# Twelve gate tiles of an encoder layer as six seven-product pairs around a state scan

## The chip, the cores and the metric

The kernel runs on one core of a Trainium2 chip. Its time is the device time of one execution in microseconds; the profile's span, from the first to the last instruction, lies about one microsecond below it. In the profile PE is TensorE's matmuls, PEld its weight loads, DVE is VectorE, ACT ScalarE, POOL GpSimd and SP SyncE, which issues the DMAs here.

## The reference

One encoder layer works on two sequences (prompt and sample) of 512 tokens and width 1024, each with 256 memory tokens, in fp32. Of the layer, this is what matters here:

```python
xn = _rmsnorm(x, p['norm_mix'][l])
h = xn @ p['w_in'][l]
u, q, k, v, xq, g = jnp.split(h, IN_SPLITS, axis=-1)
y_s5 = _s5_branch(u, ...)                      # a scan over time, forward and backward, then a GLU
y_diff = _diff_attention(q, k, v, ...)
y_x = _cross_attention(xq, mk, mv)
for n in range(N_BRANCH):
    term = jax.nn.sigmoid(g[..., n * D_MODEL:(n + 1) * D_MODEL]) * (branches[n] @ p['w_up'][l, n])
    merged = term if merged is None else merged + term
x = x + merged @ p['w_out'][l]
gate, up = jnp.split(_rmsnorm(x, p['norm_ffn'][l]) @ p['w_ffn_in'][l], 2, axis=-1)
return x + (jax.nn.silu(gate) * up) @ p['w_ffn_out'][l]
```

The three gates are 3 x 1024 columns of `h`: 24 tiles of 128 columns, each for 1024 tokens (both sequences) and a contraction over 1024.

## The kernel before

Activations lie with features on the partitions and the 1024 tokens along the free axis. Every fp32 operand is split in a high part that TensorE takes as fp32r and a low part that is the rest (`split`: a copy on ScalarE, line 134, and a subtraction on VectorE, line 135, or 138 with a scale). A product is three matmuls: high by high, high by low, low by high. A tile of 128 output columns for both sequences thus takes 8 (contraction) x 2 (sequences) x 3 = 48 matmuls of 128x512.

The core is one program for a scheduler that orders each engine's instructions at build time: of what is ready, what stands earlier in the program goes first. `issue_after` puts instructions of an engine behind a given one; `PE.on` keeps TensorE in program order (in both attention stages). Before the attention TensorE is free in order, so work that stands later fills waits.

The stages are: memory keys and values; the norm of x, whose split parts `xh[k]`, `xl[k]` (eight each, 1024 tokens) stay until the end of the attention; the projection `u`; the state-space branch (`s5_gen`), the gates around it; the GLU; cross attention; differential attention with its projections; merges; output projection; feed-forward.

Gates: `gates(n)` takes the next n of 24 tiles (`todo`), computes each with `proj`, applies tanh (line 410) and stores it in `gD` (line 411). In the attention stages `gate_units` does the same in pieces of 6 matmuls, from a queue (`queue`, `fill`) that fills the waits for the softmax: `fill(n)` asks for n such matmuls. `NG` and the calls between say how many tiles stand where: 7 ahead of the scan, 3 more, 3 between parts of the scan, 2 between its outputs, 3 behind the GELU (`gates(NG[2])`), 2 in the cross attention, 4 in the differential attention.

The state-space branch is a generator that the main program advances with `next(s5)`. It computes parameters (VectorE), input weights (`input_weights`: products at lines 1551 to 1553, transposes), output weights (`output_weights`: the same products, then matmuls at line 1597 and small stores at 1603 to 1605), the scan's inputs (line 1626), then the scan: 62 steps of four VectorE operations of 128x128 (lines 1641 to 1644), each step on the result of the one before. In the kernel before it yields at the steps in `SCAN`, with a gate's split put between. Behind the scan come four outputs (`x2` copied at 1677 and 1678, matmuls at 1685 to 1687, copies at 1688, eight stores each at 1692), which need the kernels and c from DRAM (`kernels_in`, `c_in`) and the tile `u_`. Then the GELU of the four z tiles (lines 502 to 514), whose tiles lie over those of the branch, and the GLU (lines 525 to 533).

The scheme with seven products in place of eight is in the kernel already, for the feed-forward: `quad_sums` forms four sums of quadrants of the activations (three on VectorE, one on GpSimd), `weights4` four sums of quadrants of two weight tiles on GpSimd (lines 1022 to 1025), and `products` and `quadrants` compute two tiles (gate and up) with seven products of 4 x 3 matmuls and add the results on VectorE out of PSUM (line 1101).

Of the kernel before, what the change touches and what calls it, by code (L numbers as in the profile page):

```python
# [10 lines left out]
F32 = mybir.dt.float32  # L11
# [27 lines left out]

NPREP = (16, 28)  # L40

NG = (7, 6, 3)

NWARM = 13

SCAN = (40, 47, 53, 60)
ROUND = 12582912.0


# [23 lines left out]
def encoder(ctx: ExitStack, tc: tile.TileContext, a, out):  # L73
# [134 lines left out]
    bD = drp.tile([3, 4, P, NT], F32, name="bD")  # L208
    gD = drp.tile([24, P, NT], F32, name="gD")
    mD = drp.tile([4, P, 2, L], F32, name="mD")  # L210
    yD = drp.tile([512, T, NS, NC], F32, name="yD")
    uD = drp.tile([512, T, NS, NC], F32, name="uD")
    kx = Ctx()
# [169 lines left out]
    for t2 in range(2):  # L383
# [9 lines left out]
        for t in range(2):  # L393
            nc.sync.dma_start(uD[(2 * t2 + t) * P : (2 * t2 + t + 1) * P], us[t])

    todo = iter(range(24))

    def behind():
# [3 lines left out]
    def gates(n):  # L402

        for _ in range(n):
            t = next(todo)
            o = proj(a["w_in"][20 + t], xh, xl)
            gt = slot("ld", name="gt")
            for s in range(NS):
                cs = slice(s * L, (s + 1) * L)
                S.activation(out=gt[:, cs], in_=o[s], func=AF.Tanh, scale=0.5)  # L410
            nc.sync.dma_start(gD[t], gt)

    next(s5)
    gates(NG[0])
    next(s5)
    gates(NG[1] + 1 - len(SCAN))
    for i in range(len(SCAN)):
        if i:
            gates(1)
        with tc.issue_after(last_s[1].ins):  # L420
            next(s5)
    for n in (0, 1, 1):
        gates(n)
        with behind():
            next(s5)
    next(s5, None)

    res_ = ExitStack()
# [73 lines left out]
    for t in range(4):  # L502
# [401 lines left out]
    for i in range(-1, n + 3):  # L904
        if i + 1 < n:
            score(i + 1)
        if i == 22:
            queue.insert(1, first_in())
        fill(10 if i < n - 1 else 16)
        if 0 <= i < n:  # L910
            turn(i)
        if 0 < i <= n and steps[i - 1][2] % 2:
            outputs(i - 1)
        fill(10)
        if 1 < i <= n + 1 and steps[i - 2][2] == 3:
            squares(i - 2)
        if i > 2 and steps[i - 3][2] == 3:
            normed(i - 3)
# [42 lines left out]
        nc.sync.dma_start(x1D[m, :, cs], x1[m][:, cs])  # L961
        sum_sq(accs[s], x1[m][:, cs], m == 0)

    last_p = None

    def quad_sums(xa_, xb_, tag="ts", third=PO):

        nonlocal last_p
        b11, b12, b21, b22 = xa_[:, 0:L], xa_[:, L:NT], xb_[:, 0:L], xb_[:, L:NT]
        t_ = slot(tag, [P, 4, L], name="ts")  # L970
        V.tensor_tensor(out=t_[:, 0], in0=b12, in1=b11, op=ALU.subtract)
        last_p = third.tensor_tensor(out=t_[:, 2], in0=b22, in1=b12, op=ALU.subtract)
        V.tensor_tensor(out=t_[:, 1], in0=b22, in1=t_[:, 0], op=ALU.subtract)
        V.tensor_tensor(out=t_[:, 3], in0=b21, in1=t_[:, 1], op=ALU.subtract)
        return t_
# [17 lines left out]
    def operands(i):  # L993
# [6 lines left out]
    H = 4 * P  # L1000

    def weights4(i):

# [406 lines left out]
def s5_gen(k):  # L1410
# [221 lines left out]
            wbs.append(input_weights(3))  # L1632
    for o in range(2, 4):
        output_weights(o)
    yield
    sv = st_t.rearrange("p r g s c -> p r (g s) c")
    l8rv, l8iv = l8r.rearrange("p r g s -> p r (g s)"), l8i.rearrange("p r g s -> p r (g s)")
    for i in range(2, NC):
        p_ = sp.tile([P, 2, G * NS], F32, tag="p_", name="p_")
        q_ = sp.tile([P, 2, G * NS], F32, tag="q_", name="q_")  # L1640
        V.tensor_tensor(out=p_, in0=sv[:, :, :, i - 1], in1=l8rv, op=ALU.mult)
        V.tensor_tensor(out=q_, in0=sv[:, ::-1, :, i - 1], in1=l8iv, op=ALU.mult)
        V.tensor_tensor(out=p_, in0=p_, in1=sv[:, :, :, i], op=ALU.add)
        V.tensor_tensor(out=sv[:, :, :, i], in0=p_, in1=q_, op=ALU.add)
# [147 lines left out]
```

## Time and profile before

| what | value |
|---|---|
| median of three runs | 1603.96 us (1602.52 to 1604.57) |
| profiled execution, span | 1603.0 us, its own time not listed apart |
| TensorE busy | 1587.1 us (99%), 7838 matmuls |
| VectorE busy | 1162.9 us (73%) |
| ScalarE busy | 640.0 us (40%) |
| GpSimd busy | 541.6 us (34%) |
| mean granted clock of TensorE | 0.997 |

A busy TensorE is not one at its peak: matmuls are pipelined, and one that lasts 0.39 us in the profile starts about 0.23 us after the one before it. Idle time of another engine costs nothing unless TensorE waits for it.

### The profile page before, as it was taken

The page shows a single profiled execution, that of the slowest core. Times are in us where ns is not written, and L with a number is a line of the kernel's source. Part 1 is how long each engine was busy: PE and PEld are TensorE (multiplying, and loading weights), DVE is VectorE, ACT ScalarE, POOL GpSimd, SP SyncE. Part 2 cuts the span into 40 slices and gives each one's busy share as a digit, 9 for nine tenths or more (in the row PEclk, how much of TensorE's full clock was granted, in tenths as well). Part 3 has the DMA queues.
Part 4 walks back from the last instruction along what each step waited for, and adds up shares of the span by engine and source line. Part 5 has one row for each costly group of instructions (what it writes and reads, how often), then busy time and mean ns, then how long its engine had stood idle before and what let it go on. Part 6 is the DMA issues. An engine that isn't in the chain of part 4 may idle for free.

```text
span 1603.0 us, 21625 instructions
## 1 busy us (share of the span) xinstructions
PE 1587.1 (99%) x7838; PEld 1314.8 (82%) x7838; DVE 1162.9 (73%) x1856; ACT 640.0 (40%) x1142; POOL 541.6 (34%) x449
## 2 busy tenths in 40 slices
PE   9999999999999999999999999999999999999997
PEld 7888788888898778778878878888888888788877
DVE  7976996076773766776465678888898778988654
ACT  6544323274652455574133443332333323233323
POOL 0010100001333220300343367676665553444653
PEclk9999999999999999999999999999999999999998
DMA  9554523576762111244454432333323223986222
GB/s 366 173 160 150 179 95 125 180 273 201 252 224 102 54 47 40 73 156 140 145 190 132 144 118 80 131 119 129 121 106 118 79 88 119 344 332 198 80 66 106
DMA packets 104891, 237.86 MB, mean 148 GB/s; under 512 B 13520, under 2 KB 45008, under 8 KB 104784
## 3 DMA queue, kind: packets, MB, share of 16 engines
q1 hardware_dynamic: 104784, 236.47, 43.1%
q8 instruction: 62, 1.02, 0.3%
q14 instruction: 45, 0.37, 0.1%
HBM read 165.16 MB, written 71.27 MB: 147 GB/s over the span
## 4 chain that ended last, share of the span: by engine, by line
PE 87%; issue 4%; DVE 3%; DMA 3%; POOL 2%; ACT 0%; SPq 0%; POOLq 0%; DVEq 0%; ACTq 0%
PE bkmm L66 75%; PE bksc L66 3%; PE bktr L66 2%; PE bkoo L66 2%; PE bktr L69 2%; DVE tl L135 1%; PE bktr L1626 1%; POOL mg L793 1%; PE bktr L1597 1%; DMA yt<-bD 1%; PE bktr L1686 0%; PE bktr L1687 0%; PE bktr L1685 0%; PE bktr L1565 0%; DMA acc<-in_w_fo 0%
## 5 line engine op out<-in xcount | busy, mean ns | idle before, releaser
L66 PE MATMUL bkmm<-xh,wh 128*128 128x512 f32 x640 | 255.4, 399 | 0.0
L66 PE MATMUL bkmm<-xh,wl 128*128 128x512 f32 x640 | 250.9, 392 | 0.0
L66 PE MATMUL bkmm<-xl,wh 128*128 128x512 f32 x640 | 250.5, 391 | 0.0
L66 PE MATMUL bkmm<-tl,wh 128*128 128x512 f32 (+1 forms) x621 | 241.2, 388 | 1.4 <-DVE tl L135 1.4
L66 PE MATMUL bkmm<-th,wl 128*128 128x512 f32 (+1 forms) x621 | 241.0, 389 | 0.9 <-DVE wl L135 0.9
L66 PE MATMUL bkmm<-th,wh 128*128 128x512 f32 (+1 forms) x621 | 241.1, 389 | 0.0
L134 ACT CAST wh<-wf 128x1024 fp32r<-128x1024 f32 (+1 forms) x134 | 117.9, 880 | 224.1 <-PE bkmm L66 179.8
L135 DVE TENSOR_TENSOR wl<-wf,wh 128x1024 fp32r<-128x1024 f32 (+1 forms) x134 | 145.1, 1083 | 50.2 <-ACT wh L134 45.7
L66 PEld LDWEIGHTS bkmm<-xh,wh 128*128 128x128 f32 x640 | 120.3, 188 | 30.3 <-issue 7.9
L66 PE MATMUL bkmm<-th,w 128*128 128x512 f32 x432 | 141.5, 392 | 2.7 <-DVE up L1101 1.0
L66 PEld LDWEIGHTS bkmm<-xh,wl 128*128 128x128 f32 x640 | 120.2, 188 | 26.7 <-issue 1.3
L66 PEld LDWEIGHTS bkmm<-xl,wh 128*128 128x128 f32 x640 | 120.4, 188 | 22.4 <-issue 0.4
L66 PEld LDWEIGHTS bkmm<-tl,wh 128*128 128x128 f32 x621 | 116.6, 188 | 25.9 <-DVE tl L135 2.1
L66 PEld LDWEIGHTS bkmm<-th,wl 128*128 128x128 f32 x621 | 116.5, 188 | 25.7 <-DVE wl L135 1.7
L66 PEld LDWEIGHTS bkmm<-th,wh 128*128 128x128 f32 x621 | 116.6, 188 | 23.9
L1165 POOL TENSOR_TENSOR up<-up,acc 128x512 f32<-128x512 f32 x44 | 83.6, 1920 | 87.8 <-DVE up L1101 87.8
L454 POOL TENSOR_TENSOR raw<-raw 128x128 f32<-128x128 f32 x28 | 15.2, 545 | 284.4 <-DVE nb L545 206.5
L66 PEld LDWEIGHTS bkmm<-th,w 128*128 128x128 f32 x432 | 80.9, 188 | 23.8 <-DVE up L1101 3.4
L793 POOL TENSOR_TENSOR mg<-mg,gl 128x1024 f32<-128x1024 f32 x16 | 43.5, 2720 | 139.0 <-DVE gl L789 139.0
L548 ACT ACTIVATE e<-bksc,nb 128x512 f32<-128x512 f32 (+1 forms) x96 | 58.8, 615 | 73.5 <-DVE nb L543 51.9
L66 PE MATMUL bkmm<-tl,w 128*128 128x512 f32 x216 | 84.2, 390 | 0.0
L66 PE MATMUL bkmm<-yh,wh 128*128 128x512 f32 x192 | 75.9, 397 | 0.8 <-ACT wh L134 0.4
(641 smaller groups left out, 3527.8 us busy)
## 6 DMA issues: line engine op xcount, KB each, us to landing
wf<-in_w_in SPq DMA_DIRECT2D x40, 512.0 KB, 3.9
wD<-hl SPq DMA_DIRECT2D x28, 512.0 KB, 2.9
w<-wD SPq DMA_DIRECT2D x28, 512.0 KB, 5.0
gD<-gt SPq DMA_DIRECT2D x24, 512.0 KB, 2.8
gl<-gD SPq DMA_DIRECT2D x24, 512.0 KB, 3.4
wf<-in_w_fg SPq DMA_DIRECT2D x22, 512.0 KB, 3.7
wf<-in_w_fu SPq DMA_DIRECT2D x22, 512.0 KB, 3.6
aD<-ac SPq DMA_DIRECT2D x22, 512.0 KB, 3.1
```

The costliest lines, as they stand in the source:

```text
L66: return self.put(self.eng.matmul(*args, **kw))
L69: return self.put(self.eng.transpose(*args, **kw))
L134: h = S.copy(hi, src)
L135: l_ = V.tensor_tensor(out=lo, in0=src, in1=hi.bitcast(F32), op=ALU.subtract)
L454: PO.tensor_tensor(out=a22, in0=a21, in1=a22, op=ALU.add)
L548: last_x = S.activation(out=e, in_=sc, func=AF.Exp, bias=nb, scale=scale, accum_out=sm)
L793: PO.tensor_tensor(out=mg[m], in0=mg[m], in1=gt, op=ALU.add)
L1165: PO.tensor_tensor(out=up, in0=up, in1=accs[s], op=ALU.mult)
L1597: PE.matmul(kp[64 * hf : 64 * hf + 48, g * 144 : (g + 1) * 144], l_[:, 2 * hf + g, :], o_[:, 4 * g4 + 2 * hf + g, :], start=(l_ is lr48), ...
L1626: PE.matmul(ps[:, g * P : (g + 1) * P], w_[:, gg * P : (gg + 1) * P], u_[:, 8 * o + gg, :], start=True, stop=True)
```

## The change

Twelve of the gate tiles are computed as six pairs. For a pair the two weight tiles and x are cut into quadrants: the two tiles are the rows, the halves of the contraction (x tiles 0 to 3 and 4 to 7) the inner index, the two sequences the columns. Seven products of 12 matmuls each, with sums of the quadrants as operands, replace eight.

- x after its norm is also stored in DRAM (`xD`, 8 stores); the second sequence's half of the parts of x tiles 0 to 3 is stored too (`b12D`, 8 stores).
- Ahead of the pairs, `xD` is loaded in four rounds, `quad_sums` forms the sums of x (three subtractions on VectorE, one on GpSimd), and they are split. One sum takes the place of the second sequence's half in `xh[i]`, `xl[i]`; the other three go to new tiles `tq`, which lie over the tiles of the branch's preparation (`rt.close()` now stands ahead of the scan). After the pairs that half is loaded back.
- For each pair `gate_weights` loads two weight tiles, forms four sums on GpSimd and splits three quadrants and four sums; `quad_gates` runs the products, adds out of PSUM with VectorE, applies tanh and stores both tiles. The split sums lie in the tile that `u_` had, so `u_` is loaded a second time behind the scan.
- The order: 4 gates, six pairs, the whole scan (which no longer yields between), 1 gate, outputs with 1 and 1 gate between, 2 gates behind the GELU. So 21 tiles stand ahead of the GLU instead of 18; the cross attention's queue has 1 gate instead of 2, the differential attention 2 in all instead of 4, and it fills with 9 instead of 10 until its step 22.

```diff
-NG = (7, 6, 3)
+NG = (4, 6, 1, 1, 1, 0, 2)
-SCAN = (40, 47, 53, 60)
...
+    for i in range(4):
+        nc.sync.dma_start(xD[:, 2 * i : 2 * i + 2, :L], xt[2][:, 2 * i : 2 * i + 2])
+        nc.sync.dma_start(xD[:, 2 * i : 2 * i + 2, L:], xt[3][i])
...
+    def gate_weights(ta, tb, sw):
+        nonlocal last_w, last_s
+        a1, a2 = (wp.tile([P, DM], F32, tag="wf", name="wf") for _ in range(2))
+        nc.sync.dma_start(a1, a["w_in"][20 + ta])
+        last_w = nc.sync.dma_start(a2, a["w_in"][20 + tb])
+        (h1, l1), (h2, l2) = (tuple(wp.tile([P, DM], F32R, tag=n_, name=n_) for n_ in ("wh", "wl")) for _ in range(2))
+        split(h1, l1, a1)
+        last_s = split(h2[:, :H], l2[:, :H], a2[:, H:])
+        s12, s34 = (slot("ld", name="ws") for _ in range(2))
+        PO.tensor_tensor(out=s12[:, :H], in0=a2[:, :H], in1=a2[:, H:], op=ALU.add)
+        PO.tensor_tensor(out=s12[:, H:], in0=s12[:, :H], in1=a1[:, :H], op=ALU.subtract)
+        PO.tensor_tensor(out=s34[:, H:], in0=a1[:, H:], in1=s12[:, H:], op=ALU.subtract)
+        PO.tensor_tensor(out=s34[:, :H], in0=a1[:, :H], in1=a2[:, :H], op=ALU.subtract)
+        last_s = split(sw[:, 0], sw[:, 1], s12)
+        last_s = split(sw[:, 2], sw[:, 3], s34)
...
+    def quad_gates(ops_, sw):
...
+        pu, pv = bank(), bank()
+        product_(pu, "A11", 0)
+        product_(pv, "A12", 1)
+        u_ = copied("nsq")
+        out_(ga[:, :L], pv, u_)
+        product_(pu, "S2", 4, start=False)
+        pv = bank()
+        product_(pv, "S1", 3)
+        u_ = copied("acc")
+        u4 = rp.tile([P, L], F32, tag="nsq", name="u4", bufs=2)
+        V.tensor_tensor(out=u4, in0=pv, in1=u_, op=ALU.add)
+        product_(pu, "S3", 5, start=False)
+        u_ = copied("acc")
+        out_(gb[:, L:], pv, u_)
+        pv = bank()
+        product_(pv, "S4", 2)
+        out_(ga[:, L:], pv, u4)
+        product_(pu, "A22", 6, start=False)
+        S.activation(out=gb[:, :L], in_=pu, func=AF.Tanh, scale=0.5)
...
+    for i in range(4):
+        for j, x_ in enumerate((xh, xl)):
+            nc.sync.dma_start(b12D[i, j], x_[i].bitcast(F32)[:, L:])
     next(s5)
     gates(NG[0])
+    ges = ExitStack()
+    open_tags(ges, side="right", tq=8, tsx=1)
+    sw = slot("su", [P, 4, DM], F32R, "sw")
+    xops = []
+    for i in range(4):
+        xa_, xb_ = slot("ld", name="xa"), slot("ld", name="xb")
+        nc.sync.dma_start(xa_, xD[:, i])
+        nc.sync.dma_start(xb_, xD[:, i + 4])
+        t_ = quad_sums(xa_, xb_, "tsx")
+        tq = [slot("tq", [P, 3, L], F32R, n_) for n_ in ("tqh", "tql")]
+        split(*tq, t_[:, 1:4])
+        split(xh[i][:, L:], xl[i][:, L:], t_[:, 0])
...
+    for _ in range(NG[1]):
+        quad_gates(xops, sw)
+    for i in range(4):
+        for j, x_ in enumerate((xh, xl)):
+            nc.sync.dma_start(x_[i].bitcast(F32)[:, L:], b12D[i, j])
     next(s5)
-    gates(NG[1] + 1 - len(SCAN))
-    for i in range(len(SCAN)):
-        if i:
-            gates(1)
-        with tc.issue_after(last_s[1].ins):
-            next(s5)
-    for n in (0, 1, 1):
-        gates(n)
+    ges.close()
+    gates(NG[2])
+    for n in NG[3:6]:
         with behind():
             next(s5)
+        gates(n)
...
-    gates(NG[2])
+    gates(NG[6])
...
-    queue += [xq[1], gate_units(), xq[2], xq[3], v_units(0, v0), gate_units(), units(a["w_in"][4], xh, xl, dq0.__setitem__)]
+    queue += [xq[1], xq[2], xq[3], v_units(0, v0), gate_units(), units(a["w_in"][4], xh, xl, dq0.__setitem__)]
...
-    queue += [qk_units(1, True), dk[1], gate_units(), qk_units(2, True), dk[2], v1_, qk_units(3, True), dk[3], gate_units(),
-              gate_units(), merges()]
+    queue += [qk_units(1, True), dk[1], gate_units(), qk_units(2, True), dk[2], v1_, qk_units(3, True), dk[3], merges()]
...
-        fill(10 if i < n - 1 else 16)
+        fill(9 if i < 22 else 10 if i < n - 1 else 16)
...
-        fill(10)
+        fill(9 if i < 22 else 10)
...
     for o in range(2, 4):
         output_weights(o)
+    rt.close()
     yield
...
-        if i in SCAN:
-            yield
     yield
 
-    rt.close()
+    u_ = slot("su", [P, G, NS * NC], name="u2_")
+    for o in range(4):
+        for j in range(8):
+            nc.sync.dma_start(u_[j * 16 : (j + 1) * 16, 8 * o : 8 * o + 8], uv[j, :, 8 * o : 8 * o + 8])
```

More of the change, by code (lines that the diff above doesn't have):

```diff
@@ L210, in encoder @@
     mD = drp.tile([4, P, 2, L], F32, name="mD")
+    xD = drp.tile([P, KD, NT], F32, name="xD")
+    b12D = drp.tile([4, 2, P, L], F32, name="b12D")
     yD = drp.tile([512, T, NS, NC], F32, name="yD")
@@ L394, in encoder, with quad_sums @@
             nc.sync.dma_start(uD[(2 * t2 + t) * P : (2 * t2 + t + 1) * P], us[t])
+    last_p = None
+    def quad_sums(xa_, xb_, tag="ts", third=PO):
+        nonlocal last_p
+        b11, b12, b21, b22 = xa_[:, 0:L], xa_[:, L:NT], xb_[:, 0:L], xb_[:, L:NT]
+        t_ = slot(tag, [P, 4, L], name="ts")
+        V.tensor_tensor(out=t_[:, 0], in0=b12, in1=b11, op=ALU.subtract)
+        last_p = third.tensor_tensor(out=t_[:, 2], in0=b22, in1=b12, op=ALU.subtract)
+        V.tensor_tensor(out=t_[:, 1], in0=b22, in1=t_[:, 0], op=ALU.subtract)
+        V.tensor_tensor(out=t_[:, 3], in0=b21, in1=t_[:, 1], op=ALU.subtract)
+        return t_
     todo = iter(range(24))
@@ L411, in gates @@
             nc.sync.dma_start(gD[t], gt)
+    H = 4 * P
+    def gate_weights(ta, tb, sw):
[13 more added lines that the diff above has]
+        last_s = split(sw[:, 2], sw[:, 3], s34)
+        res = {"A11": (h1[:, :H], l1[:, :H]), "A12": (h1[:, H:], l1[:, H:]), "A22": (h2[:, :H], l2[:, :H])}
+        for i, nm in enumerate(("S1", "S2", "S3", "S4")):
+            hs = slice(i % 2 * H, i % 2 * H + H)
+            res[nm] = sw[:, i // 2 * 2, hs], sw[:, i // 2 * 2 + 1, hs]
+        return res
@@ new lines, in quad_gates, with product_, copied, out_ @@
+    def quad_gates(ops_, sw):
+        ta, tb = next(todo), next(todo)
+        w = gate_weights(ta, tb, sw)
+        def product_(ps, nm, o, start=True):
+            nonlocal last_mm
+            wh, wl = w[nm]
+            for k in range(4):
+                th, tl = ops_[k](o)
+                ws_ = slice(k * P, (k + 1) * P)
+                more = {} if start else {"skip_group_check": True}
+                PE.matmul(ps, wh[:, ws_], th, start=(start and k == 0), stop=False, **more)
+                PE.matmul(ps, wh[:, ws_], tl, start=False, stop=False, **more)
+                last_mm = PE.matmul(ps, wl[:, ws_], th, start=False, stop=(k == 3), **more)
+        def copied(tag):
+            t_ = rp.tile([P, L], F32, tag=tag, name="u" + tag, bufs=2)
+            S.copy(t_, pu)
+            return t_
+        ga, gb = slot("ld", name="ga"), slot("ld", name="gb")
+        def out_(dst, p_, u_):
+            V.tensor_tensor(out=dst, in0=p_, in1=u_, op=ALU.add)
+            S.activation(out=dst, in_=dst, func=AF.Tanh, scale=0.5)
+        pu, pv = bank(), bank()
[17 more added lines that the diff above has]
+        S.activation(out=gb[:, :L], in_=pu, func=AF.Tanh, scale=0.5)
+        nc.sync.dma_start(gD[ta], ga)
+        nc.sync.dma_start(gD[tb], gb)
@@ new lines, in encoder @@
+    xops = []
[7 more added lines that the diff above has]
+        split(xh[i][:, L:], xl[i][:, L:], t_[:, 0])
+        lo_, hi_ = slice(0, L), slice(L, NT)
+        xops.append(lambda o, i=i, tq=tq: [(x_[i][:, lo_], x_[i + 4][:, lo_], x_[i + 4][:, hi_], x_[i][:, hi_], *(t[:, j] for j in range(3)))[o]
+                                           for x_, t in zip((xh, xl), tq)])
@@ L685, in encoder @@
     xq = {h: xq_units(h) for h in range(1, 4)}
-    queue += [xq[1], gate_units(), xq[2], xq[3], v_units(0, v0), gate_units(), units(a["w_in"][4], xh, xl, dq0.__setitem__)]
+    queue += [xq[1], gate_units(), xq[2], xq[3], v_units(0, v0), units(a["w_in"][4], xh, xl, dq0.__setitem__)]
     PE.on = True
@@ L962, in out_tile @@
         sum_sq(accs[s], x1[m][:, cs], m == 0)
[L964 to L975, printed above, removed]
     def quad_room(i):
@@ L998, in operands @@
         return quad_split(i, xa_, xb_, quad_sums(xa_, xb_))
-    H = 4 * P
     def weights4(i):
```

## The prediction

> **What bounds the kernel now.** I read the page first: busy time by engine, then TensorE's row of the slices.
>
> ```profile
> span 1603.0 us, 21625 instructions
> PE 1587.1 (99%) x7838; PEld 1314.8 (82%) x7838; DVE 1162.9 (73%) x1856; ACT 640.0 (40%) x1142; POOL 541.6 (34%) x449
> PE   9999999999999999999999999999999999999997
> ```
>
> TensorE is busy in every slice, so a matmul that is left out is worth its full issue interval, as long as the others can feed what is left. The change sits around the state scan, so I cut that stage with the table of windows: scan, outputs, wait for the outputs, GELU.
>
> ```profile
> 161.00:262.70 101.70, 101.70 (x488) 82.20 (x487) 97.75 (x262) 25.09 (x51) 5.93 (x8) 1.00 0.39 131
> 262.70:297.00 34.30, 34.30 (x217) 30.82 (x216) 8.74 (x8) 15.73 (x17) 0.00 (x0) 1.00 0.62 190
> 297.00:324.00 27.00, 27.00 (x154) 23.62 (x154) 1.22 (x1) 4.60 (x8) 0.00 (x0) 1.00 0.51 159
> 324.00:351.40 27.40, 27.40 (x122) 22.68 (x122) 25.26 (x47) 19.11 (x28) 0.00 (x0) 1.00 0.69 251
> ```
>
> VectorE (third busy figure) works 97.75 of 101.7 us while the scan runs, 10 of the next 61, and 25 of 27 in the GELU; TensorE never waits, because gate tiles fill it, and GpSimd (fifth) does next to nothing. The stage thus has two clocks: the gates' matmuls, and a serial VectorE chain from the scan to the GLU. The price of a gate comes from the chain that ended last.
>
> ```profile
> 282.86 10.90 PE bkmm L66 x48
> ```
>
> 48 matmuls take 10.90 us, 0.227 us each; the 0.39 us in the groups is the pipelined duration, not the interval.
>
> **What the change takes away.** A pair of gates needs 96 matmuls now and 7 x 12 = 84 after: 12 less, 12 x 0.227 = 2.73 us, times six pairs 16.4 us. The feed-forward stage already runs this scheme; its stores of finished pairs give a second price.
>
> ```profile
> 1035.16 0.33 SPq L1168 DMA_DIRECT2D aD<-ac  x1
> 1053.93 0.33 SPq L1168 DMA_DIRECT2D aD<-ac  x1
> ```
>
> 18.77 us a pair against 2 x 10.90 is 3.03 us, 18.2 us in all. I take 16.4 and keep 18.2 for the range.
>
> **What it puts on VectorE.** First the scan's own price.
>
> ```profile
> 161.04 0.39 DVE L1641 TENSOR_TENSOR p__1960<-st,l8r 128x128 f32<-128x128 f32 x1
> ...
> 207.49 0.39 DVE L1644 TENSOR_TENSOR st<-p__2116,q__2117 128x128 f32<-128x128 f32 x1
> ...
> 208.92 0.39 DVE L1644 TENSOR_TENSOR st<-p__2122,q__2123 128x128 f32<-128x128 f32 x1
> ...
> 262.56 0.39 DVE L1644 TENSOR_TENSOR st<-p__2686,q__2687 128x128 f32<-128x128 f32 x1
> ```
>
> A step lasts 208.92 - 207.49 = 1.43 us, 62 steps 88.7 us, yet the scan took 262.95 - 161.04 = 101.9. The rest is 13 operations of 1.22 us put between its steps:
>
> ```profile
> L135 DVE TENSOR_TENSOR wl<-wf,wh 128x1024 fp32r<-128x1024 f32 x8 | 9.8, 1221 | 0.0
> ```
>
> these eight and five products of the same width, for the preparation's last group. (101.9 - 88.7) / 13 = 1.0 us each: an operation between scan steps fills 0.2 us of the scan's dependency gaps. The prices of the added kinds:
>
> ```profile
> L1022 POOL TENSOR_TENSOR ws<-wf 128x512 f32<-128x512 f32 x16 | 27.8, 1738 | 41.6 <-DMA wf<-in_w_fu 33.3 <-ACT ac L1164 8.4
> L1166 DVE SCALAR_TENSOR_TENSOR ac<-ac,gf 128x512 f32<-128x512 f32 x32 | 40.0, 1249 | 8.5 <-ACT ac L1164 8.5
> L1101 DVE TENSOR_TENSOR up<-bkmm,u 128x512 f32<-128x512 f32 x32 | 21.8, 680 | 1.8 <-PE bkmm L66 1.8
> L138 DVE SCALAR_TENSOR_TENSOR hl<-raw,hl 128x512 fp32r<-128x512 f32 x12 | 21.3, 1775 | 0.0
> L1274 POOL TENSOR_TENSOR y<-y,up 128x512 f32<-128x512 f32 x6 | 7.8, 1292 | 7.5 <-DVE up L1101 7.5
> 350.88 0.68 DVE L138 SCALAR_TENSOR_TENSOR zl<-zy,zh 128x512 fp32r<-128x512 f32 x1
> ```
>
> The first four are from the feed-forward stage, where GpSimd works beside VectorE. A pair adds three 1024-wide subtractions (1.22), one 512-wide (0.68) and four adds out of PSUM (0.68): 7.1 us, less eight times 0.2, so 5.4; six pairs 32. The sums of x are four rounds of three subtractions and a 512-wide low part (0.68 each) and a 1536-wide one (1.22 x 1.5 = 1.8): 4.5 less five times 0.2, so 3.5; in all 14. With the scan, five products and three single gates (1.0 each), VectorE needs 88.7 + 32 + 14 + 8 = 143 us from 161 on: the scan would end at 304 instead of 263.
>
> GpSimd's part comes on top: 24 weight sums and 4 of x, where it did nothing before. A 512-wide operation with both inputs in SBUF takes VectorE 0.68 alone, but 1.25 (L1166) or 1.78 us (L138) beside GpSimd, and GpSimd's add 1.74 instead of 1.29; one with an input in PSUM stays at 0.68. Per GpSimd operation VectorE so loses 0.57 to 1.1 us, at most the whole 1.29. I take 0.8, nearer to L1166 because part of VectorE's work reads PSUM and the scan has gaps of its own: 28 x 0.8 = 22 us, and the scan ends at 326.
>
> **Does the cover reach?** From the scan's end to the GLU:
>
> ```profile
> 262.98 3.71 ACT L1677 COPY x<-st 64x2048 f32<-64x2048 f32 x2 [6.52 <-DVE st L1644]
> 271.99 0.38 PE L1685 MATMUL bktr<-u__1212,w__2711 128*128 128x128 f32 x2
> ...
> 277.34 0.39 PE L1685 MATMUL bktr<-u__1212,w__2724 128*128 128x128 f32 x2
> gl<-gD SPq DMA_DIRECT2D x24, 512.0 KB, 3.4
> 324.33 1.29 DVE L506 SCALAR_TENSOR_TENSOR zy<-zu,vec,zy 128x1024 f32<-128x1024 f32 x1 [12.21 <-DMA zy<-yD]
> 351.10 0.59 ACT L410 ACTIVATE gt<-bkmm 128x512 f32<-128x512 f32 x1
> ```
>
> One copy (3.71 / 2 = 1.9), four outputs back to back (5.35 each, from 271.99 to 277.34), a load of 512 KB (3.4) and the GELU (324.33 to 351.56, 27.2): 54 us, since the GELU's tiles lie over those that the last output reads. Before, 88 us passed, stretched by gates put between the outputs; that slack pays for most of the added work. TensorE's cover ended at 351.4 with the 18th gate; now 14 gates (152.6) become six pairs (6 x 84 x 0.227 = 114.4) and five gates (54.5): 16.3 us more, 367.7. A further 8.2 us is the three quarters of four GLU products that need only the first three z tiles (36 x 0.227). So the GLU waits if the scan ends later than 367.7 + 8.2 - 54 = 322: at 326 it is 4 us. The deciding loss is (322 - 304) / 28 = 0.64 us per GpSimd operation.
>
> **The start of the first pair.** Four gates stand ahead of the pairs instead of seven, and the tiles for the sums' parts lie over the scan's preparation.
>
> ```profile
> 173.61 0.34 SPq L411 DMA_DIRECT2D gD<-gt  x1
> 190.11 0.41 PE L1597 MATMUL bktr<-cxi,li 128*48 128x144 f32 x4
> 193.26 0.43 SPq L1605 DMA_DIRECT2D gD<-gk  x1
> ```
>
> The fourth gate is stored at 173.6, the last preparation matmul runs at 190.1 and its last store goes out at 193.3. In between TensorE has A11, A12 and S4 of the first pair, A11 of the second and what S2 and S1 can do without the last quarter: 24 + 12 + 12 + 18 matmuls, 15 us, and a microsecond of preparation, so to 190. The last part of the sums is split about 196 (3 to land, as the 512 KB load above, 3 to split, less some 3 because the scan no longer stands in between). That is a wait of 0 to 17 us; I take 5. It delays TensorE's cover, not VectorE's chain, so of it and the GLU's 4 us only the larger counts: 5.
>
> **The rest.** Around the scan SyncE gets 8 restores, 32 reloads of u and, no longer early because their room is the pairs', 16 loads of the first kernels and 4 of c. Eight stores of y took
>
> ```profile
> 316.36 3.95 SPq L1692 DMA_DIRECT2D yD<-y__3002  x8
> ```
>
> 0.49 us each, so these 60 need 30 us behind the last pair (about 295): 325, level with the scan's end and in front of the weights of single gates. I add nothing, up to 3 us. The 8 stores of x and 8 of its parts near 62 us go ahead of the u loads in the same queue; 0.5, up to the 4 that eight stores take above. Both attention stages lose fill. In the cross attention the queue held 384 units (six tiles of 48, v of 96) and the loop asks for 364 (35 steps of 10, 14 extra); now it holds 336, so the last two steps run bare:
>
> ```profile
> L134 ACT CAST xpTh<-bktr 128x256 fp32r<-128x256 f32 x28 | 10.3, 369 | 6.8 <-PE bktr L69 6.6
> L135 DVE TENSOR_TENSOR xpTl<-bktr,xpTh 128x256 fp32r<-128x256 f32 x28 | 11.7, 418 | 1.6 <-ACT xpTh L134 1.6
> 692.61 1.22 DVE L138 SCALAR_TENSOR_TENSOR yl<-yt,yh 128x1024 fp32r<-128x1024 f32 x1
> 706.04 0.39 PE L66 MATMUL bkmm<-yh,wh 128*128 128x512 f32 x1
> ```
>
> at least 0.8 us of split per step stands open: 2, between 1 and 4. In the differential attention the two gates ahead of the merges go. The merges' last operand was ready at 693.8, 12 us before its first matmul; without the gates that slack is used up: 1, between 0 and 5.
>
> Sum: 1603.0 - 16.4 + 5 + 0.5 + 2 + 1 = 1595.1 span. The median of the runs, 1603.96, is 0.96 above the profiled span; I forecast 1596.
>
> **The rivals.** A, slower: GpSimd's adds hold VectorE for their full 1.29 us. Then the scan ends at 304 + 36 = 340, 18 us behind the point where the GLU waits: 1603 - 16.4 + 18 + 3.5 + 1 = 1609. For it speaks that nearly all of VectorE's work here reads two SBUF inputs, and L138's 1.78; against it L1166's 1.25 and that the feed-forward stage hides as much. [...] B, no change: the preparation frees its tiles late, TensorE waits 13 us at the first pair, and the GLU's wait vanishes behind it: 1603 - 16.4 + 13 + 3.5 + 1 = 1604. C, faster still: both waits hide, 1603 - 16.4 + 1 to 3 + 1 = 1590.
>
> **Chances.** Forecast (1592 to 1600) 0.41, C 0.20, A 0.26, B 0.13. Some 0.2%, 3 us, is what a measurement can tell from no change. That gives faster 0.61, same 0.13, slower 0.26. The range runs from 1588 (18.2 us saved, 2 lost) to 1610 (A with an attention bound); the likeliest case alone is 1592 to 1600.
>
> **What would show it.** TensorE has 72 fewer matmuls; six pairs of 19 us each lie between about 175 and 295; scan steps beside GpSimd's weight sums stretch from 1.43 towards 2.2 us; the last L1644 stands near 326; TensorE idles at most 5 us before the first S2 and before L526's products. A scan end near 340 with TensorE idle before the GLU would prove A, a gap of over 10 us near 180 to 196 B. It is wrong altogether if TensorE waits inside the pairs, for adds queued behind scan steps.

## The result, and the profile after

| | before | after |
|---|---|---|
| median of four runs | 1604.26 us (1602.52 to 1604.57) | 1684.7 us (1680.49 to 1687.39) |
| profiled span | 1603.0 us | 1685.6 us |
| mean granted clock | 0.997 | 0.973 |

The ratio of the times is 1.0501 (95% interval 1.0485 to 1.0517): 80 us slower, where 8 us faster was forecast, and far outside the range. First the page of the kernel after: busy time, then the slices of TensorE and of its clock.

```profile
span 1685.6 us, 21730 instructions
...
PE 1597.2 (95%) x7766; PEld 1314.2 (78%) x7766; DVE 1232.6 (73%) x1912; ACT 667.1 (40%) x1180; POOL 582.9 (35%) x477
...
PE   9999378998799999998999999999999999999997
...
PEclk9999679999899999999999999999999999999998
```

The 72 matmuls are gone (7838 to 7766), worth 16.4 us. Against that TensorE idles 1685.6 - 1597.2 = 88.4 us instead of 15.9, 72.5 more, and it is busy 10.1 us longer with less to do: the matmuls that are left cost 10.1 + 16.4 = 26.5 us more. 72.5 + 26.5 - 16.4 = 82.6 us, the whole difference of the spans. A page with TensorE at 99% has become one with holes: slices 5 to 7 (169 to 295 us), 10 and 11 (379 to 464). The clock's row dips in slices 5, 6 and 11, where the holes are largest.

The windows of the prediction, in the kernel after, and two behind them (TensorE's busy time and matmuls come first after the window's length, then weight loads, VectorE, ScalarE, GpSimd; the clock follows GpSimd):

```profile
161.00:262.70 101.70, 61.46 (x275) 46.98 (x274) 98.81 (x193) 30.93 (x57) 28.50 (x24) 0.75 0.27 92
262.70:297.00 34.30, 28.30 (x112) 21.32 (x111) 33.34 (x78) 12.92 (x19) 5.37 (x4) 0.95 0.26 93
297.00:324.00 27.00, 25.21 (x100) 20.58 (x101) 24.49 (x45) 8.53 (x14) 5.58 (x4) 0.87 0.28 100
324.00:351.40 27.40, 27.40 (x122) 22.72 (x121) 9.03 (x11) 9.13 (x14) 5.08 (x4) 1.00 0.57 207
365.00:400.00 35.00, 30.56 (x181) 26.84 (x180) 4.00 (x4) 8.46 (x10) 0.00 (x0) 0.95 0.82 238
420.00:460.00 40.00, 29.47 (x110) 21.85 (x109) 27.86 (x51) 22.74 (x33) 0.00 (x0) 0.88 0.76 270
```

In the first window TensorE runs 275 matmuls where it ran 488, while VectorE is as full as before. So 40 of the idle microseconds lie there; some 8 more beside the rest of the scan, 4.4 and 10.5 behind the pairs. The waits of TensorE over the whole span, by what ended them:

```profile
PE bkmm L65 <- ACT sw L133: 26.6, 2, 26.3
PE bkmm L65 <- DVE sw L134: 9.4, 4, 3.4
PE bkmm L65 <- ACT zh L136: 5.7, 3, 2.9
...
PE bktr L1781 <- DMA c_r<-cD: 4.2, 1, 4.2
...
PE bkmm L65 <- DVE tql L134: 2.4, 1, 2.4
```

One wait of 26.3 us stands above all: the first pair's S2, for the split sum of weights `sw`. Four shorter ones wait for the low part of `sw`, one in the first pair, three in later ones. `tql` is the last round of x, `zh` the GLU, `c_r` the outputs. In the same list of the kernel before no wait is longer than 1.2 us.

**Inside the first pair.** TensorE's first S2 in the timeline, the first cast of x's parts (ScalarE), the first and the last of the four splits (VectorE), and GpSimd's second sum of x and first sum of weights:

```profile
216.07 0.80 PE L65 MATMUL bkmm<-tqh,sw 128*128 128x512 f32 x1 [26.32 <-ACT sw L133]
...
190.83 1.47 ACT L133 CAST tqh<-ts 128x1536 fp32r<-128x1536 f32 x1
...
196.65 1.76 DVE L134 TENSOR_TENSOR tql<-ts,tqh 128x1536 fp32r<-128x1536 f32 x1
...
233.39 1.75 DVE L134 TENSOR_TENSOR tql<-ts,tqh 128x1536 fp32r<-128x1536 f32 x1
...
198.49 1.26 POOL L408 TENSOR_TENSOR ts<-xb,xa 128x512 f32<-128x512 f32 x1 [12.48 <-DVE tql L134]
...
209.06 1.79 POOL L442 TENSOR_TENSOR ws<-wf 128x512 f32<-128x512 f32 x1 [0.68 <-DVE ts L407]
```

The first part is split about 191 to 198; the prediction had the last one split by then (196). There are four rounds, and they pass through one buffer (`tsx=1`): the sums of the next begin when the split of the last has ended ("<-DVE tql"). The three rounds behind the first take (233.39 - 196.65) / 3 = 12.2 us each on average, and the last part is ready at 235. GpSimd makes the pair's sums of weights only from 209 on, behind three of the rounds in its own order, in the four `ld` tiles that x is loaded into as well. S2 starts when the cast of these sums is done (`sw`, ScalarE, from 214.97 on); the last part of x comes later still and makes one of the shorter waits (`tql`).

**The other pairs.** Stores of the second tile of the first, fourth and sixth pair, the last scan step, the start of the second load of u, and the first output's copy:

```profile
248.55 0.33 SPq L501 DMA_DIRECT2D gD<-gb  x1
...
320.91 0.32 SPq L501 DMA_DIRECT2D gD<-gb  x1
...
358.69 0.38 SPq L501 DMA_DIRECT2D gD<-gb  x1
...
316.75 0.39 DVE L1738 TENSOR_TENSOR st<-p__3016,q__3017 128x128 f32<-128x128 f32 x1
...
349.59 9.00 SPq L1744 DMA_DIRECT2D u__3084<-uD  x19
...
380.15 0.58 ACT L1783 COPY y__3167<-bktr 128x512 f32<-128x512 f32 x1 [5.48 <-PE bktr L1782]
```

Beside the scan a pair takes (320.91 - 248.55) / 3 = 24.1 us; behind it (358.69 - 320.91) / 2 = 18.9, the forecast's 19. The scan ends at 317.1, 9 us earlier than forecast, and nothing starts at its end: the outputs' chain starts behind the last S4 (u at 349.6, in the tile of `sw`) and the last pair (c and the kernels, in the tiles of the x sums, issued from 367.6 on); the first output stands 21.5 us behind the last pair's store.

### The profile page after: what moved, and what is told of

The parts are those of the page before. It is cut to its first block, busy times and chain, and to the rows that moved or that the text cites. A ratio compares the mean times of both kernels' runs of the same rounds, so it can differ in the third digit from the quotient of the medians.

```text
span 1685.6 us, 21730 instructions
## 1 busy us (share of the span) xinstructions
PE 1597.2 (95%) x7766; PEld 1314.2 (78%) x7766; DVE 1232.6 (73%) x1912; ACT 667.1 (40%) x1180; POOL 582.9 (35%) x477
## 4 chain that ended last, share of the span: by engine, by line
PE 80%; DVE 12%; DMA 3%; issue 2%; ACT 1%; SPq 1%; POOL 0%; POOLq 0%; DVEq 0%; ACTq 0%
PE bkmm L65 69%; PE bktr L65 3%; PE bksc L65 2%; PE bkoo L65 2%; PE bktr L68 2%; DVE tl L134 2%; DVE st L1738 1%; DVE wl L134 1%; PE bktr L1719 1%; DMA c_n<-cD 1%; DVE ts L409 0%; PE bktr L1658 0%; PE bktr L1690 0%; DMA bD<-sg 0%; DMA rs<-in_rope_s 0%
## 5 line engine op out<-in xcount | busy, mean ns | idle before, releaser
L65 PE MATMUL bkmm<-xh,wh 128*128 128x512 f32 x496 | 200.3, 404 | 2.7 <-DVE ga L478 1.7
L65 PE MATMUL bkmm<-xh,wl 128*128 128x512 f32 x496 | 195.6, 395 | 1.3 <-DVE wl L134 1.3
L65 PE MATMUL bkmm<-xl,wh 128*128 128x512 f32 x496 | 195.8, 395 | 0.0
L65 PEld LDWEIGHTS bkmm<-xh,wh 128*128 128x128 f32 x496 | 94.1, 190 | 28.3 <-issue 6.9
L65 PEld LDWEIGHTS bkmm<-xh,wl 128*128 128x128 f32 x496 | 93.9, 189 | 22.5 <-DVE wl L134 1.8
L65 PEld LDWEIGHTS bkmm<-xl,wh 128*128 128x128 f32 x496 | 94.2, 190 | 16.8 <-issue 0.2
L65 PEld LDWEIGHTS bkmm<-th,w 128*128 128x128 f32 x432 | 81.0, 188 | 21.5 <-DVE up L1194 3.1
L1257 ACT ACTIVATE ac<-gf 128x512 f32<-128x512 f32 x44 | 27.8, 633 | 171.3 <-DMA aD<-ac 90.0
```

Of the source, the lines that this page charges most:

```text
L65: return self.put(self.eng.matmul(*args, **kw))
L1257: last_t = S.activation(out=ac[:, cs], in_=gf, func=AF.Tanh, scale=0.5)
```

## The experiments

All times are compared with runs of the kernel before on the same chip (1603.8 to 1604.2 us). The kernel after is 1684.7, with a spread of its own of 1680.5 to 1687.4, so a difference from it of a few microseconds says little.

**All sums on VectorE.**

```diff
-        t_ = quad_sums(xa_, xb_, "tsx")
+        t_ = quad_sums(xa_, xb_, "tsx", V)
...
-        PO.tensor_tensor(out=s12[:, :H], ...)   # and the three behind it
+        V.tensor_tensor(out=s12[:, :H], ...)
```

> All 28 sums that GpSimd made (24 of weights, 4 of x) are made on VectorE instead. Theory Q (queues): TensorE is late because the first pair waits for the four rounds of the x sums, which start only when the preparation's tiles come free (about 189 us) and pass one by one through a single buffer, with scan steps queued between them on VectorE. Then GpSimd matters little: the wait before the first S2 stays at 20 us or more, the rounds lose only GpSimd's own queue, and the time falls by 5 to 15 us, to 1670-1680. Theory L (lock): GpSimd's adds block VectorE, and VectorE's total work is what makes everything late; VectorE then gains 28 x 0.97 - 28 x 0.68 = 8 us and no step is stretched; scan steps beside weight sums fall from 5.3 to 1.4 us, the scan ends near 300 instead of 317, and if this is the main cause the time falls by 40 us or more, below 1645.

Measured: 1665.95 us, ratio 1.038 (1.035 to 1.0411), 18.7 us less than with GpSimd. The first S2 and the second and the last pair's stores in the timeline, then a window beside the scan:

```profile
213.00 0.80 PE L65 MATMUL bkmm<-tqh,sw 128*128 128x512 f32 x1 [23.91 <-ACT sw L133]
...
261.50 0.33 SPq L501 DMA_DIRECT2D gD<-gb  x1
...
339.90 1.24 SPq L501 DMA_DIRECT2D gD<-gb  x1
```

```profile
222.00:300.00 78.00, 72.98 (x312) 57.47 (x311) 76.23 (x179) 29.67 (x43) 0.00 (x0) 1.00 0.27 94
```

The first wait stays (23.9 us), so it isn't GpSimd's. But the pairs come every 19.6 us ((339.90 - 261.50) / 4), also beside the scan, and the clock beside them is full. Neither theory gave this size: GpSimd's sums cost the pairs' pace, and the scan's end hardly at all (313 instead of 317). Half of the gain is there when the first pair is stored (239.3 instead of 248.55), the rest comes up to the last.

**The scan behind the sums.**

```diff
-    next(s5)
+    with tc.issue_after(last_x[1].ins):    # the low part of the last x sum
+        next(s5)
```

> The whole scan is put behind the split of the last x sum on VectorE; nothing else changes. Theory Q (queues): a round of sums falls from 12 to about 7 us, the first S2 runs at about 205 us instead of 216, the wait before it falls from 26 to 10-15 us, and the pairs end near 340 instead of 358; but the scan starts near 200 instead of 161 and ends near 335. Time 1665 to 1680. Theory L (lock, VectorE's total work decides): VectorE idles between the rounds, its work ends later than 317, and the time rises, to 1700 or more. Theory B (the late release of the preparation's tiles alone makes the wait): first S2 as late as before, time 1685 or more.

Measured: 1690.07 us, ratio 1.0531 (1.05 to 1.0561). VectorE's splits of the first three rounds, and the first S2:

```profile
193.63 1.76 DVE L134 TENSOR_TENSOR tql<-ts,tqh 128x1536 fp32r<-128x1536 f32 x1 [11.74 <-DMA gD<-gk]
...
200.58 1.76 DVE L134 TENSOR_TENSOR tql<-ts,tqh 128x1536 fp32r<-128x1536 f32 x1 [1.59 <-ACT tqh L133]
...
209.66 2.61 DVE L134 TENSOR_TENSOR tql<-ts,tqh 128x1536 fp32r<-128x1536 f32 x1 [1.58 <-ACT tqh L133]
...
210.63 0.80 PE L65 MATMUL bkmm<-tqh,sw 128*128 128x512 f32 x1 [22.76 <-ACT sw L133]
```

Expectation Q fails in part: without one scan step between them the second and third round still take 7 and 9 us, and S2 comes only 5.4 us earlier, and the time doesn't fall. The steps queued between were not the main thing; the dependent chain of a round is. And the scan, now from 220 to 358, lies beside nearly all of the six pairs, which ate the gain. The first split waited for the last `gk` store to land: the low part's tile is free only at 193.6.

**Seven gates ahead.**

```diff
-NG = (4, 6, 1, 1, 1, 0, 2)
+NG = (7, 6, 0, 0, 0, 0, 2)
```

> Three of the gates that stood behind the pairs stand ahead of them (seven, six pairs, none between the outputs, two in the GELU). TensorE then has work until about 209 us, well after the preparation's tiles come free at 189. Theory B (the late release makes the first pair wait): the wait before the first S2 falls from 26 to under 8 us. Theory Q (the serial chain of the sums makes it): the sums take the buffers that the gates used, so they start only behind the seventh gate, and a wait of 20 us or more stays, now near 215 to 240. Then three gates of cover are missing behind the pairs and the time is 1690 to 1720; by B it is 1655 to 1680.

```profile
237.31 0.79 PE L65 MATMUL bkmm<-tqh,sw 128*128 128x512 f32 x1 [22.98 <-ACT sw L133]
```

Measured: 1691.41 us, ratio 1.0539 (1.0509 to 1.057). TensorE waits 23 us here too, though the room has been free for nearly 20 when the sums begin: the sums' first subtraction runs at 212, by the code since their loads share the `ld` tiles with the gates, and one sum replaces a part of x that the gates still read. So the late release (rival B) alone doesn't make the wait; Q holds. The three gates that moved are missing behind the pairs, where TensorE now waits 26.6 us for the GLU's `zh` in one piece (2.9 in the kernel after), so the time rises as Q expected.

**Half a scan.** The loop runs to `NC // 2`; 32 of the 62 steps are left out (the expectation's 30 are those that stay).

> Half of the scan's steps are left out (30 of 62; the state of the later steps is not formed). VectorE has 32 x 1.43 = 46 us less to do and the scan ends 50 us earlier or more. Theory C (the outputs start when the pairs end, because their tiles and the second load of u lie over those of the pairs): the outputs still start about 25 us behind the last pair's store, and the time falls only by what the pairs gain, 5 to 30 us (1655 to 1680). Theory S (the scan's end sets the GLU, as the prediction has it): the outputs start at the scan's end, the GLU no longer waits, and the time falls by 50 us or more.

```profile
242.60 0.39 DVE L1738 TENSOR_TENSOR st<-p__2824,q__2825 128x128 f32<-128x128 f32 x1
...
344.85 0.34 SPq L501 DMA_DIRECT2D gD<-gb  x1
...
366.31 0.59 ACT L1783 COPY y__2975<-bktr 128x512 f32<-128x512 f32 x1 [5.48 <-PE bktr L1782]
```

Measured: 1669.56 us, ratio 1.0403 (1.0353 to 1.0453). The scan ends 74 us earlier, the first output 13.8 earlier, again 21.5 us behind the last pair's store, and the time falls by 15. Theory C holds: the scan's end does not set the outputs; the pairs' end does. The pairs, nearly all behind the shortened scan, come every 19.1 us ((344.85 - 249.34) / 5, from the first pair's store to the last's), though GpSimd makes their sums here too: it takes GpSimd's sums and the scan together to slow them.

**The second load of u from ScalarE's queue** (`nc.sync` to `nc.scalar` in its loop), and **in eight pieces**:

```diff
-    for o in range(4):
-        for j in range(8):
-            nc.sync.dma_start(u_[j * 16 : (j + 1) * 16, 8 * o : 8 * o + 8], uv[j, :, 8 * o : 8 * o + 8])
+    for j in range(8):
+        nc.sync.dma_start(u_[j * 16 : (j + 1) * 16], uv[j])
```

> The changed kernel with the second load of u (32 pieces) issued by ScalarE's queue instead of SyncE's. Theory C (behind the last pair a chain of loads runs in SyncE's order: 32 pieces of u, about 0.47 us each, then c and the kernels; the outputs wait for it): c and the kernels are issued about 15 us earlier, the first output runs at about 366 us instead of 378, TensorE's waits between 365 and 460 us fall from 15 us to under 8, and the time falls by 6 to 14 us, to 1671-1679. Theory S (the scan's lateness sets the GLU) and a theory by which the transfers themselves are the limit (the DMA engines are 95% busy there): no change, 1681 to 1687.

> The changed kernel with the second load of u in 8 pieces of 256 KB instead of 32 of 64 KB, still from SyncE. Theory C (SyncE's row of loads behind the last pair holds the outputs): u takes some 4 us of SyncE instead of 16, c and the kernels follow 12 us earlier, the first output runs at about 366 us instead of 378, TensorE's waits between 365 and 460 us (14 us) fall by half or more, and the time falls by 6 to 14 us against 1684.7. (With u on ScalarE's queue TensorE waited 10 us for u itself: those pieces were issued late, behind ScalarE's other work; that doesn't speak against C.) Theory D (the DMA engines' transfers are the limit there, not the issue): the first output comes as late as before and the time stays within 4 us.

```profile
PE bktr L1780 <- DMA u__3084<-uD: 10.2, 1, 10.2
...
PE bktr L1779 <- DMA w__3109<-gD: 5.8, 1, 5.8
```

From ScalarE's queue: 1692.71 us, ratio 1.055 (1.0534 to 1.0566), slower, since TensorE now waited 10.2 us for u itself (the first row is of that run). It was not ScalarE's other work that made u late: between 349.7 and 377.2, when the 32 loads are issued (349.6 to 367.5 from SyncE's queue), that is about 3 us. The first eight loads of kernels on SyncE's queue, issued meanwhile, started over 10.8 us (358.6 to 369.4) instead of 5.8 (368.5 to 374.3); why both rows were slower is not shown. In eight pieces: 1680.14 us, ratio 1.0474 (1.0457 to 1.0492), 4.6 us less, with an interval that overlaps that of the kernel after. The first load of c is issued 10 us earlier (357.7 instead of 367.6), but the first output's copy stands at 379.1 instead of 380.2, not at 366 as C expected, and TensorE now waits 5.8 us for the kernels (second row). So the order of issue is not what holds the outputs. D fits better, but no run tried the transfers by themselves.

**The attention's side alone, and the added stores alone**, both on the kernel before:

```diff
-NG = (7, 6, 3)
+NG = (7, 6, 6)
...                                   # the queue and fill lines of the change
```

> The kernel before with the change's attention side alone: three gates stand behind the GELU instead of in the two attention stages, and the differential attention fills with 9 up to step 22. No pair, no x sums. The prediction costs this at 3 us (2 in the cross attention, 1 at the merges): 1607. The traces of before and after, read from the end of the GELU to the first store of x1, say 9 us: 1611 to 1614. If the loss seen there is only a consequence of the late scan stage, 1604 to 1606.

> The kernel before with only the 16 added stores of x and its parts (nothing reads them). The prediction costs them at 0.5 us, with up to 4: 1604.5. The trace after shows gates two to four stored 1.8 to 2.5 us later than before: 1605.5 to 1607.

```profile
PE bktr L69 <- DVE e L849: 2.2, 1, 2.2
PE bkoo L66 <- DVE xpTl L135: 1.9, 1, 1.9
```

The attention: 1616.8 us, ratio 1.0075 (1.0062 to 1.0087), 12.7 us; the profiled execution lost 8.0, of which four rows of its waits show 6.9: xpT at the last steps of the cross attention (2.9), `yl` and `e` in the differential attention (4.0). In this run as in the change, the gate that stays in the cross attention's queue is the first of the two, behind `xq[1]`; the diff of the change shows the second. The stores: 1606.08 us, ratio 1.0013 (1.0004 to 1.0021), 2 us.

**The x sums left out**, first with the splits kept, then with their tiles too:

```diff
-        t_ = quad_sums(xa_, xb_, "tsx")
-        split(*tq, t_[:, 1:4])
-        split(xh[i][:, L:], xl[i][:, L:], t_[:, 0])
+        split(*(t[:, :2] for t in tq), s3[0])          # the same widths, from xa_ and xb_
+        split(*(t[:, 2] for t in tq), s3[1][:, 0])
+        split(xh[i][:, L:], xl[i][:, L:], s3[1][:, 1])
```

> The changed kernel without the sums of x: quadrants of x are split in their place (the loads, the same amount of splits and the sums of weights stay; the gates of the pairs are then not the reference's). Theory Q (four serial rounds of three dependent subtractions, split and the next round's start through one buffer): a round falls from 10-12 us to about 4, the first S2 runs at about 203 us instead of 216, the last quarter of the parts is ready near 208 instead of 235, and the time falls by 15 to 30 us, to 1655-1670. Theory W (the weights' sums on GpSimd are what the first S2 waits for, whatever the x sums do): it waits for the weights' parts as late as before, time above 1675.

> The changed kernel without any sums, splits or tiles of x for the pairs: S1 to S4 multiply the parts of x that are there (the pairs' gates are then not the reference's). The pairs' weight sums stay, as do the reloads behind the pairs; but the outputs' tiles no longer lie over the pairs', so c and the kernels of the first two outputs are loaded during the pairs, and only u comes behind them. Theory Q: the wait before the first S2 (26 us with the sums, 18.5 with the splits alone) falls under 8, the scan ends near 300. Theory C (loads behind the last pair hold the outputs): TensorE's waits between the last pair and the GLU's end (14 us) fall under 6, and the time is 1630 to 1650. Theory D (those waits come from the y stores and the GELU, whatever was loaded early): they stay at 10 us or more, and the time is 1650 to 1662.

The first S2 with the splits alone; then, with neither, the stores of the first and the fourth pair and the last, the first output's copy, and two windows behind:

```profile
204.77 0.80 PE L65 MATMUL bkmm<-tqh,sw 128*128 128x512 f32 x1 [18.52 <-ACT sw L133]
```

```profile
208.03 0.38 SPq L501 DMA_DIRECT2D gD<-gb  x1
...
282.13 0.32 SPq L501 DMA_DIRECT2D gD<-gb  x1
...
334.63 0.37 SPq L501 DMA_DIRECT2D gD<-gb  x1
...
338.44 0.58 ACT L1775 COPY y__3099<-bktr 128x512 f32<-128x512 f32 x1 [1.32 <-PE bktr L1774]
```

```profile
365.00:400.00 35.00, 35.00 (x180) 29.88 (x180) 10.87 (x15) 10.69 (x15) 0.00 (x0) 1.00 0.66 222
400.00:460.00 60.00, 49.42 (x214) 38.88 (x213) 40.45 (x80) 34.94 (x59) 3.07 (x6) 0.97 0.56 193
```

Splits alone: 1672.52 us, ratio 1.0428 (1.0407 to 1.0449), 12 us less, between what Q and what W expected; S2 comes 11.3 us earlier and still waits 18.5, for the weights' sums, which by the code share tiles and engines with the loads of x. Neither: 1647.91 us, ratio 1.0271 (1.0254 to 1.0288), 36.8 us less; the first pair is done 40.5 us earlier, and no wait of TensorE between 183 and 215 us is over 2.4. Its pairs beside the scan keep 24.7 us ((282.13 - 208.03) / 3): the slow pace is GpSimd's sums beside the scan, not x. With c and the kernels loaded early the first output follows 3.8 us behind the last pair and the window to 400 has no hole (C); the window to 460 still has 10.6 us of them, at the GELU (D). Both theories have a part.

**A repaired order, twice.** The first sum goes to DRAM and takes its place in x only behind more gates, so that single gates run beside the rounds; four pairs; all sums on VectorE.

```diff
-        split(xh[i][:, L:], xl[i][:, L:], t_[:, 0])
+        nc.sync.dma_start(t0D[i], t_[:, 0])
...
+    gates(4)                                # second version: six gates ahead, two here
+    for i in range(0, 4, 2):                # load t0D, split into xh[i], xl[i]
...
```

> A repaired order, to test whether the causes together explain the loss: the first sum of x goes to DRAM and takes the place of x's half only after four more gates, which run beside the rounds of sums; so eight single gates stand ahead of four pairs, and TensorE has work until about 220 us. All sums on VectorE; the second load of u from ScalarE's queue. Theory Q with C (first pair's serial rounds, GpSimd's share, loads behind the pairs): no wait over 5 us before the first S2, the pairs end near 300, the scan near 300, and the time is 1600 to 1615 (10.9 us saved by four pairs, 9 lost in the attention, 2 at the start, the rest behind the pairs). If the pairs are slow for another reason (the clock, TensorE's own order), the time stays above 1640.

> The repaired order once more, mended where its trace showed new waits: six gates, the rounds of sums, two gates, then four pairs (in the first repaired order TensorE waited 17.7 us for a tanh queued behind the sums' casts on ScalarE, and 16.5 us for u from ScalarE's queue); u in 8 pieces from SyncE. If those waits were all that was wrong, the time falls from 1663.6 by about 13 + 12 and some 6 of the clock, to 1625-1640. What is left against 1604 is then the attention's 12 us, 2 of the stores and the waits behind the pairs, less 10.9 that four pairs save. Above 1650: the pairs and what follows them cannot be fed even so.

Rows of the waits of the first version, then of the second:

```profile
PE bkmm L65 <- ACT gt L428: 17.7, 1, 17.7
PE bktr L1787 <- DMA u__3077<-uD: 11.3, 1, 11.3
```

```profile
PE bkmm L65 <- ACT sw L133: 9.4, 5, 6.5
PE bktr L1786 <- DMA w__3102<-gD: 7.7, 1, 7.7
```

First: 1663.62 us, ratio 1.0371 (1.0357 to 1.0385), far above the 1600 to 1615 expected. The wait for the sums was gone, but a tanh queued on ScalarE behind their casts held TensorE as long, and u came late from ScalarE. Second: 1646.93 us, ratio 1.0268 (1.0253 to 1.0283), 16.7 us better and 7 above its expectation. The longest wait before a first S2 is 6.5 us, so the rounds of x sums were rightly named for that wait, though the two versions change several things at once. 43 us remain against the kernel before, which no version tried beats.

## Why the prediction was wrong

**Right:** the saving. 72 matmuls less, and a pair that is fed takes 18.9 to 19.6 us. **About right, in part by luck:** VectorE's list of work. The scan ended at 317, forecast 326, but the forecast put the work of all six pairs ahead of its end, and that of the last two (the splits of their sums and their additions out of PSUM, the first at 318.95) ran behind it.

**The first pair's wait, forecast 5 with bounds 0 and 17,** is the term that failed most: 26.3 us in one piece, with two of 2.7 and 2.4 behind it. The release of the preparation's tiles was placed well (190, measured 191 to 193.6). The failing step is "the last part of the sums is split about 196": it let one landing and one split follow the release, as if the rounds before were done by then. None could end before the release, since all write into those tiles, and each waits for the one before to leave the single buffer. So the last split began at 233.4: one split and three rounds of 12.2 us had to be added to 190. The 4.5 us a round that the prediction itself lists as VectorE's work, with GpSimd's and ScalarE's share in the chain, would have pointed to it. The step also had no place for the pair's own sums of weights, and the 26.3 us end with their cast: with the x sums left out S2 still waited 18.5 us for them, and only with x's parts gone altogether did the wait vanish. That run gives back 36.8 us, a part of it by the early loads behind the pairs.

**GpSimd's sums.** A stretch of the timeline of after: the first of four sums on GpSimd (to 283.45), and the starts of the scan step beside them and of the next:

```profile
278.00 1.44 POOL L442 TENSOR_TENSOR ws<-wf 128x512 f32<-128x512 f32 x1 [19.69 <-DMA wf<-in_w_in]
...
278.42 1.19 DVE L1735 TENSOR_TENSOR p__2920<-st,l8r 128x128 f32<-128x128 f32 x1
...
283.74 0.39 DVE L1735 TENSOR_TENSOR p__2926<-st,l8r 128x128 f32<-128x128 f32 x1
```

The step takes 5.32 us instead of 1.43: 0.97 us lost per GpSimd operation, against 0.8 taken and rival A's 1.29. In kind the trace is as A has it: each of the step's four VectorE operations, 0.37 to 0.39 us in the next step, takes 1.19 to 1.46 us and ends 0.17 to 0.25 us behind a GpSimd operation, and GpSimd's four take 1.33 to 1.44 us. But A's consequence did not come: the scan was not later, and the half scan shows that its end decides nothing here. What came is close to what the prediction named as making it wrong altogether: TensorE waits inside the pairs, though for the low parts of `sw` and not for additions (0.9, 2.4 and 3.4 us in the second, third and fourth pair). GpSimd's sums themselves were not late: those of the fence above were cast only from 293.1 on. In the wait of 3.4 us that follows, the low part stands behind scan steps in VectorE's order, from 295.1 to 297.5. So it is VectorE that is behind. That GpSimd's sums put it there is shown by the runs with half a scan (19.1 us a pair) and with all sums on VectorE (19.6, against 24.1); that this loss alone is worth the 18.7 us of the time is not shown, since 28 x (0.97 - 0.68) is only 8 us of VectorE's work.

**Behind the pairs.** "I add nothing, up to 3" counted 30 us of loads, but from a last pair at 295 and beside a scan that would end at 325. The pairs ended at 359, and the loads' room is the pairs': so the outputs wait for the pairs' end and 21.5 us more, not for the scan. The break-even at a scan end of 322 thus compared the wrong event.

**The small terms.** The attention was forecast at 3 us and costs 12.7 alone (8 in its profile); the added stores 0.5, measured 2 (0.6 to 3.4).

**A term that was missing: the clock.** The forecast priced every matmul at 0.227 us. Three windows of after, around one wait of 2.42 us in the third pair:

```profile
271.20:273.50 2.30, 0.00 (x0) 0.00 (x0) 2.27 (x6) 1.72 (x2) 0.00 (x0) 0.93 0.58 239
273.60:276.20 2.60, 2.60 (x6) 2.12 (x7) 2.60 (x6) 0.00 (x0) 0.00 (x0) 0.50 0.24 60
276.60:280.00 3.40, 3.40 (x16) 2.77 (x16) 3.37 (x6) 1.22 (x2) 2.00 (x2) 1.00 0.16 65
```

Behind the wait TensorE runs at a granted 0.50 for some 3 us, 6 matmuls in 2.6 us, and then at 1.00 again, 16 in 3.4. Behind each of the ten waits of 2.4 us or more in this trace (2.40 to 26.32) TensorE ran at 0.50 for a stretch, so each is paid again in part; one more such stretch, 597 to 601, stands behind waits of 0.96 and 1.85 us. In the stretches at 0.50 TensorE is busy 43 us in all; at 1.00 that work would take about half, by the 0.43 and 0.21 us a matmul of the last two windows, so an estimate of 21 of the 26.5 us of slower matmuls is the clock's. It was not tried by itself.

Alone, the parts measure 36.8 (x's parts, early loads included), 18.7 (GpSimd), 12.7 (attention) and 2 (stores): 70.2, less 16.4 saved is 53.8 of the 80. They overlap and don't add strictly, so what is left of the 80 is not placed. Some of it lies behind the pairs, where the early loads closed one gap and the one at the GELU (10.6 us) stayed open.

## What to carry to other kernels

When new tiles lie over old ones, count from the release: every operation that fills them, in each round, and through how many buffers; the sum is a start time, not a load on an engine. Ask of what follows which tile it waits for: here the outputs were tied to the pairs' end by room, and the end of the scan, on which the argument was built, was no event at all. The seven-product scheme here pays its 2.7 us a pair only where VectorE and the fill have room (18.9 to 19.6 us a pair, against 24.1 beside the scan); this kernel, at 99% of TensorE before, paid for its holes twice, once idle and, behind those of 2.4 us or more, once at a granted 0.50.

## What the runs showed of the hardware

- A single wait of 2.42 us (to 273.6 in the kernel after) was followed by about 3 us at a granted clock of 0.50; in the kernel before, where TensorE was busy without a break from 161 to 351, the clock stayed at 1.00 through the whole stage.
- Four 128x128 operations on VectorE beside four 128x512 sums on GpSimd took 5.32 us instead of 1.43 (278.4 to 283.7 in the kernel after), while GpSimd's sums took 1.33 to 1.44 us: each of the small ones ended 0.17 to 0.25 us behind one of the large.
- With the 32 loads of u on ScalarE's queue, the first eight loads of kernels on SyncE's started over 10.8 us (358.6 to 369.4) instead of 5.8 (368.5 to 374.3), and TensorE waited 10.2 us for u.
